# Branch B of a hybrid attention block: four heads of a key-value group in one value product, one transpose for their meta weights, one order of the keys

## The chip, the cores and the metric

The kernel runs on one core of one Trainium2 chip. The time is the device time of one execution in microseconds (us); the median of three runs before the change is 1888.18 us (1886.59 to 1889.76). A profile is one execution of the program taken by the hardware profiler. In it PE is TensorE (matmuls), PEld its weight loads, DVE is VectorE, ACT is ScalarE, POOL is GpSimd, and SP is SyncE, which issues the DMAs. L1261 is line 1261 of the kernel before.

## The reference

One encoder layer is applied to a prompt of 2048 tokens and a sample of 512, each with 16 learned meta tokens ahead of it. A projection gives queries, keys, values and gates for two attention branches. Branch A attends over a grid. Branch B is what changes here: windowed attention with eight query heads and two key-value heads, so that four query heads share one head's keys and values (a key-value group).

```python
s_band = einsum('bnqkgd,bnckd->bnkgqc', qr, k_band) * scale + band_bias    # 3 blocks of 128 keys
s_meta = einsum('bnqkgd,bmkd->bnkgqm', qr, km) * scale + meta_bias         # 16 meta keys
p = softmax(concatenate([s_band, s_meta, sink_col], axis=-1), axis=-1)     # a sink logit per head
o_real = (einsum('bnkgqc,bnckd->bnqkgd', p[..., :C], v_band)
        + einsum('bnkgqm,bmkd->bnqkgd', p[..., C:C + N_META], vm))
```

The output of each branch is multiplied by a gate, projected, gated again, added, and projected once more; a final norm follows.

## The kernel before

All numbers are float32. A matmul at this precision is made from a high and a low part of each operand (type fp32r, one pass of TensorE each): w = wh + wl, u = uh + ul, and wh·uh + wh·ul + wl·uh is summed in PSUM (mm3, lines L146 to L148). Splitting an operand is a cast on ScalarE (the high part) and a subtraction on VectorE or GpSimd (the low part).

Up to 985 us of the profile the kernel projects the input (line L848 above all). Then the attention stretch begins. It goes through five windows of 512 tokens (window 0 is the sample). In each window come 32 units of branch A, then 16 units of branch B. Units of B are the function unit_b(w, gh, n, i): window w, key-value group gh, query block n of 128 tokens, and i, which picks two of the group's four heads. Between the units' own instructions dense projections are put in to keep TensorE at work (the generators dense_pa, dense_pb, dense_out, last_gates; function fill), six matmuls of 512 columns at a time.

A unit is a generator of stages, and the loop at L1557 calls the stages of several units in turn. In a step of unit i it calls: the loads of unit i + 4; the scores of unit i + 2; the normalising of unit i + 1; some dense work; the transposes of unit i; some dense work; the value products of unit i - 1. TensorE's instructions stay in this order. The order on VectorE, ScalarE, GpSimd and SyncE is chosen by the framework's scheduler.

The stages of a B unit, for its two heads:

- Loads. The keys' tile kt has 18 columns ahead (16 meta keys, a column for the sink, a pad), then two or three blocks of 128, then the 16 meta keys once more. The bias tile has a copy of its first columns at its end too. The first query block of a sequence has a bias tile of its own (bb0).
- Scores. Two matmuls per head (L1217, L1218) into the PSUM tile s; VectorE adds the bias and takes the row maximum (L1042, two rows of the profile: the operation, and the read of its sum); ScalarE takes the exponential and its sum (L1049). Head 0 has its meta keys at the end, head 1 at the start, so that in the tile prs the two heads' meta columns lie side by side.
- Normalising. VectorE inverts the sums (L1053) and scales one head (L1060); ScalarE scales the other (L1058).
- Transposes. TensorE transposes each block of 128 keys of each head (L1237) and the 32 meta columns of the two heads together (L1240) into PSUM tiles tp. ScalarE casts them to the high part ph (L1244), VectorE subtracts for the low part pl (L1245). ph and pl have 14 places of 128 columns; alternate units use places 0 to 5 and 6 to 11. The meta weights go to a tile pms of 96 rows (high, low, high): two casts (L1254, L1256) and a subtraction (L1255).
- Value products. For each block of keys, a matmul of the high part (L1261; 256 columns, two heads of 128 queries; v holds 64 columns high and 64 low) and one of the low part (L1266). Ahead of the last low one stand the meta products (L1264), one per head, 128 columns each, with weights vms[:, gh, h, :] of 96 rows and 64 columns.
- The upper half of the sum is copied (L1268) and added to the lower (L1271) into y32. After block 3 GpSimd multiplies by the gate z (L1274), and y_split makes high and low parts.

Of the kernel before, what the change touches and what calls it, by code (L numbers as in the profile page):

```python
# [17 lines left out]
P = 128  # L18
# [77 lines left out]
def encoder_block(ctx: ExitStack, tc: tile.TileContext, xT, x_end, w_in, w_pa, w_pb, w_o, norm_g, final_g,  # L96
# [940 lines left out]
    HALF = 416  # L1037
# [31 lines left out]
    def unit_a(w, p, h, g, sh):  # L1069
# [49 lines left out]
        pr = at.tile([P, 2 * HALF], F32, tag="pr", name="pr", bufs=3)[:, :WTOK]  # L1119
# [45 lines left out]
    def unit_b(w, gh, n, i, sh):  # L1165
# [12 lines left out]
        if n == 0 and i == 0:  # L1178
            q = sh["q"] = ld.tile([P, 2, 2, WTOK], F32R, tag="q", name="q")
            for j in range(2):  # L1180
                move(q[:, j], qb_d[w, p + j].rearrange("(h d) i t -> (d i) h t", h=2))
            bt = sh["b"] = ld.tile([P, 2, 2, EXTRA + 3 * P + N_META], F32, tag="ba", name="bb")
            for j in range(2):
                move(bt[:, j, :, : EXTRA + 3 * P], bias_b[p + j])
                move(bt[:, j, 0, EXTRA + 3 * P :], bias_b[p + j][:, 0, :N_META])
        if n == 0 and first:
            bt0 = sh["b0", i] = ld.tile([P, 2, EXTRA + 2 * P + N_META], F32, tag="b0", name="bb0")
            move(bt0[:, :, : EXTRA + 2 * P], bias_b0[p])
            move(bt0[:, 0, EXTRA + 2 * P :], bias_b0[p][:, 0, :N_META])
# [3 lines left out]
        if i == 0:  # L1193
            kt = sh["k"] = ld.tile([P, 2, EXTRA + 3 * P + N_META], F32R, tag="kd", name="kbt")
            move(kt[:, :, EXTRA : EXTRA + nbk * P],
                 kb_d[gs].rearrange("d j i t -> (d j) i t")[:, :, b0 : b0 + nbk * P])
            move(kt[:, :, :EXTRA], kbm_d[gs].rearrange("d j i t -> (d j) i t"))
            move(kt[:, :, ncol : ncol + N_META], kbm_d[gs].rearrange("d j i t -> (d j) i t")[:, :, :N_META])
        kt, q, z = sh["k"], sh["q"][:, i], sh.get(("z", i))
# [3 lines left out]
        y32 = sh["y", i]  # L1203
        bt = sh["b0", i] if first else sh["b"][:, i]
        prs = at.tile([P, 2 * HALF], F32, tag="pr", name="prs", bufs=3)
        cols = slice(HALF - ncol, HALF), slice(HALF, HALF + ncol)
        k0 = HALF - ncol + EXTRA - N_META, HALF + EXTRA
        if nbk == 2 and not first:
            nc.vector.tensor_copy(bt[:, 0, ncol : ncol + N_META], bt[:, 0, :N_META])
        sm = sums_of()  # L1210
        for h in range(2):
            if h and (gh, n, i) == (0, 0, 0):
                yield
            s = ps_s.tile([P, WTOK], F32, tag="s", name="s")

            ks = slice(N_META * (1 - h), N_META * (1 - h) + ncol)
            nc.tensor.matmul(s[:, :ncol], q[:, h, qs], kt[:, 0, ks], start=True, stop=False)  # L1217
            nc.tensor.matmul(s[:, :ncol], q[:, h, qs], kt[:, 1, ks], start=False, stop=True)  # L1218
            nm = scores_max(s, ncol, bt[:, h, ks])
            exps(prs[:, cols[h]], s[:, :ncol], nm, sm[:, h : h + 1])  # L1220
        yield
        rd = inverse(sm)
        for h in range(2):
            normalise(prs[:, cols[h]], prs[:, cols[h]], rd[:, h : h + 1], on_act=h == 1)
        yield
        slots = [("k", j) for j in range(nbk)] + [("m", 0)]
        parts = []
        c0 = 6 * ((2 * n + i) % 2)
        for half in range(0, len(slots), 2):
            tp = ps_p.tile([P, WTOK], F32, tag="tp", name="tp")  # L1230
            part = slots[half : half + 2]
            nk = sum(1 for t, _ in part if t == "k")
            for m, (t, j) in enumerate(part):
                c = 2 * m * P
                if t == "k":
                    for h in range(2):
                        nc.tensor.transpose(tp[:, c + h * P : c + (h + 1) * P],  # L1237
                                            prs[:, k0[h] + j * P : k0[h] + (j + 1) * P], ident)
                else:
                    nc.tensor.transpose(tp[: 2 * N_META, c : c + P], prs[:, HALF - N_META : HALF + N_META], ident)  # L1240
            if nk:
                x = slice(c0 + 2 * half, c0 + 2 * half + 2 * nk)
                tb = tp[:, : nk * 2 * P].rearrange("p (b t) -> p b t", t=P)
                nc.scalar.copy(ph_[:, x], tb)  # L1244
                nc.vector.tensor_sub(pl_[:, x], tb, f32(ph_[:, x]))  # L1245
            for m, (t, j) in enumerate(part):
                c = slice(2 * m * P, 2 * (m + 1) * P)
                if t == "k":
                    x = slice(c0 + 2 * (half + m), c0 + 2 * (half + m) + 2)
                    parts.append((j, *(t[:, x].rearrange("p b t -> p (b t)") for t in (ph_, pl_))))  # L1250
                else:
                    pm = pms[(2 * n + i) % 2]
                    tm = tp[:32, c.start : c.start + P]
                    nc.scalar.copy(pm[0:32], tm)  # L1254
                    nc.vector.tensor_sub(pm[32:64], tm, f32(pm[0:32]))  # L1255
                    nc.scalar.copy(pm[64:96], f32(pm[0:32]))  # L1256
        yield
        o = ps_o.tile([P, WTOK], F32, tag="o", name="ob")
        for m, (j, hi, lo) in enumerate(parts):
            vb = sh["v"][:, (b0 - tlo) // P + j, :]  # L1260
            nc.tensor.matmul(o[:, : 2 * P], vb, hi, start=(m == 0), stop=False, skip_group_check=True)  # L1261
            if m == nbk - 1:
                for h in range(2):
                    nc.tensor.matmul(o[:64, h * P : (h + 1) * P], vms[:, gh, h, :], pms[(2 * n + i) % 2], start=False,  # L1264
                                     stop=False, skip_group_check=True)
            nc.tensor.matmul(o[:64, : 2 * P], vb[:, :64], lo, start=False, stop=m == nbk - 1, skip_group_check=True)  # L1266
        ol = at.tile([64, WTOK], F32, tag="ol", name="ol", bufs=1)[:, : 2 * P]
        nc.scalar.copy(ol, o[64:128, : 2 * P])  # L1268
        for h in range(2):
            hs = slice(64 * h, 64 * h + 64)  # L1270
            nc.vector.tensor_add(y32[hs, qs], o[:64, h * P : (h + 1) * P], ol[:, h * P : (h + 1) * P])  # L1271
        if n == 3:
            eng = nc.vector if w == NWIN - 1 and gh else nc.gpsimd
            eng.tensor_mul(y32, y32, z)  # L1274
            y_split("b", w, p, y32, eng)
# [253 lines left out]
    pms = [yp.tile([96, P], F32R, tag=f"pms{i}", name=f"pms{i}") for i in range(2)]  # L1529
    vms = yp.tile([96, 2, 2, 64], F32R, tag="vms", name="vms")  # L1530
# [3 lines left out]
    with tc.manual_schedule(engines={E.PE}):  # L1534
# [17 lines left out]
        vbm = vbm_d.rearrange("m g (h f) -> m g h f", h=2)  # L1552
        for h in range(2):
            for r, part in ((0, 0), (32, 0), (64, 1)):
                move(vms[r + 16 * h : r + 16 * h + 16, :, h], vbm[:, :, part, :])
        next(units[0][2])
        for i in range(N):  # L1557
# [12 lines left out]
            fill(share)  # L1570
            next(units[i][2])
# [3 lines left out]
            if i:  # L1575
# [111 lines left out]
```

## Time and profile before

| what | value |
|---|---|
| median of three runs | 1888.18 us |
| span of the profiled execution (first to last instruction) | 1881.7 us |
| what lies between the two | 6.5 us |
| TensorE busy | 1855.9 us, 99% |
| weight loads busy (beside the matmuls) | 1583.0 us, 84% |
| VectorE, ScalarE, GpSimd busy | 70%, 61%, 39% |
| granted TensorE clock | 0.999 of full |

The page has no time of its own for the profiled execution; its span stands 6.5 us under the median of the runs, and what lies around the span is the start and the end of the execution.

In a group's row stand: line, engine, operation, output tile <- input tiles, partitions x columns, the count; then busy us, mean ns of one; then the idle time of the engine just before them and what ended it. In a timeline row stand start, length, engine, line, operation, tiles, shape, and the count of like rows that were merged. In a row of waits stand the total in us, the times and the longest. TensorE pipelines its instructions and their ends are modelled, so that rows overlap one another and the mean of a group is longer than the distance between two starts.

### The profile page before, as it was taken

How to read it: one execution, taken by the hardware profiler on the slowest of the kernel's cores; microseconds unless marked ns; L12 is line 12 of the kernel's file. 1: busy time of each engine (PE TensorE's matmuls, PEld its weight loads, DVE VectorE, ACT ScalarE, POOL GpSimd, SP SyncE). 2: the span in 40 equal slices, each digit the busy share in tenths (PEclk: the TensorE clock that was granted, in tenths of full speed). 3: DMA queues.
4: the chain of work that ended last, by engine and by line, in shares of the span. 5: the costliest groups of instructions: out<-in, count | busy, mean ns of one | idle time of the engine just before them, and what ended most of it. 6: DMA issues, size and time to landing. Idle time of an engine off the chain costs nothing. (4 is left out here: it accounts for less than half of the span.)

```text
span 1881.7 us, 29782 instructions
## 1 busy us (share of the span) xinstructions
PE 1855.9 (99%) x9797; PEld 1583.0 (84%) x9797; DVE 1320.6 (70%) x2961; ACT 1145.5 (61%) x2528; POOL 730.0 (39%) x558
## 2 busy tenths in 40 slices
PE   8999999999999999999999999999999999999998
PEld 6898888888888888888888888888888888888887
DVE  8886657556477565444457888878787887888874
ACT  6454444444365443444456797797789788878932
POOL 2005443323202233322324435656744763685420
PEclk9999999999999999999999999999999999999999
DMA  7667756544296777744258878977985996798383
GB/s 268 234 175 295 207 171 193 211 175 179 84 348 219 235 216 200 209 138 161 104 197 310 273 217 266 304 213 249 316 280 179 320 315 225 222 311 260 119 299 135
DMA packets 290385, 424.83 MB, mean 226 GB/s; under 512 B 117416, under 2 KB 162040, under 8 KB 288696
## 3 DMA queue, kind: packets, MB, share of 16 engines
q1 hardware_dynamic: 289944, 422.93, 69.5%
q8 instruction: 78, 1.28, 0.3%
q14 instruction: 75, 0.61, 0.1%
q10 hardware_dynamic: 288, 0.01, 0.0%
HBM read 303.46 MB, written 119.39 MB: 225 GB/s over the span
## 5 line engine op out<-in xcount | busy, mean ns | idle before, releaser
L208 POOL TENSOR_TENSOR wt<-wraw,wt 128x512 fp32r<-128x512 f32 x164 | 213.1, 1318 | 265.9 <-ACT wt L207 265.8
L848 PE MATMUL pa<-u,wt 128*128 128x512 f32 x1008 | 242.5, 389 | 0.0
L848 PE MATMUL pa<-u,x 128*128 128x512 f32 x984 | 236.9, 390 | 1.2 <-ACT u L859 1.1
L207 ACT CAST wt<-wraw 128x512 fp32r<-128x512 f32 x312 | 177.9, 619 | 74.8 <-PE mm L148 35.3
L848 PEld LDWEIGHTS pa<-u,wt 128*128 128x128 f32 x1008 | 189.0, 188 | 39.2
L848 PEld LDWEIGHTS pa<-u,x 128*128 128x128 f32 x984 | 184.3, 188 | 40.6 <-ACT u L859 2.2
L819 POOL TENSOR_TENSOR s<-wraw,raw 128x512 f32<-128x512 f32 x40 | 58.3, 1458 | 265.5 <-DVE x L208 265.5
L146 PE MATMUL mm<-u,wt 128*128 128x512 f32 (+2 forms) x416 | 150.4, 362 | 7.8 <-ACT u L334 7.2
L814 POOL TENSOR_TENSOR s<-raw 128x512 f32<-128x512 f32 x40 | 58.3, 1456 | 250.0 <-DMA raw<-in_w_in_dram 245.0
L148 PE MATMUL mm<-u,wt 128*128 128x512 f32 (+2 forms) x416 | 146.6, 352 | 2.4 <-DVE wt L208 2.4
L147 PE MATMUL mm<-u,wt 128*128 128x512 f32 (+2 forms) x416 | 146.6, 352 | 1.3 <-DVE u L335 1.3
L208 DVE TENSOR_TENSOR wt<-wraw,wt 128x512 fp32r<-128x512 f32 x148 | 107.2, 762 | 47.2 <-ACT wt L207 47.0
L848 PE MATMUL pe<-u,wt 128*128 128x512 f32 x504 | 121.3, 390 | 0.0
L848 PE MATMUL pc<-u,wt 128*128 128x512 f32 x504 | 121.1, 389 | 0.0
L848 PE MATMUL pe<-u,x 128*128 128x512 f32 x480 | 115.3, 389 | 0.0
L848 PEld LDWEIGHTS pc<-u,wt 128*128 128x128 f32 x504 | 94.6, 188 | 19.6
L848 PEld LDWEIGHTS pe<-u,wt 128*128 128x128 f32 x504 | 94.4, 188 | 19.6
L1139 DVE TENSOR_TENSOR pl<-tp,ph 128x384 fp32r<-128x384 f32 (+6 forms) x160 | 94.8, 593 | 20.2 <-ACT ph L1138 17.7
L1138 ACT CAST ph<-tp 128x384 fp32r<-128x384 f32 (+6 forms) x160 | 81.7, 510 | 43.4 <-PE tp L1135 41.9
L146 PE MATMUL pso<-mh,wt 128*128 128x512 f32 x256 | 107.1, 418 | 0.0
L827 POOL TENSOR_TENSOR s<-wraw,s 128x512 f32<-128x512 f32 x40 | 55.4, 1384 | 131.6 <-DVE wt L208 126.3
L848 PEld LDWEIGHTS pe<-u,x 128*128 128x128 f32 x480 | 90.1, 188 | 18.7
(258 smaller groups left out, 5017.0 us busy)
## 6 DMA issues: line engine op xcount, KB each, us to landing
wraw<-in_w_in_dram SPq DMA_DIRECT2D x86, 512.0 KB
qa<-evq SPq DMA_DIRECT2D x20, 1024.0 KB
raw<-in_w_in_dram SPq DMA_DIRECT2D x40, 512.0 KB
q<-qa SPq DMA_DIRECT2D x20, 1024.0 KB
wraw<-in_w_o_dram SPq DMA_DIRECT2D x32, 512.0 KB
kbt<-kb SPq DMA_DIRECT2D x32, 384.0 KB
qb<-evq SPq DMA_DIRECT2D x20, 512.0 KB
ka<-evk SPq DMA_DIRECT2D x20, 512.0 KB
```

The lines of the kernel that those rows point to most:

```text
L146: nc.tensor.matmul(ps, wh, uh, start=first, stop=False)
L147: nc.tensor.matmul(ps, wh, ul, start=False, stop=False)
L148: nc.tensor.matmul(ps, wl, uh, start=False, stop=last)
L207: nc.scalar.copy(h, r)
L208: low[0] = (eng or lo_eng[0]).tensor_sub(l, r, f32(h)).ins
L814: eng.tensor_add(s1, a21, a22)
L819: eng.tensor_sub(s3, a11, a21)
L827: eng.tensor_sub(s4, a12, s2)
L848: nc.tensor.matmul(ps, wt[:, a, s], u[:, b, kk, :], start=first and kk == 0 and i == 0, stop=kk == 3 and i == 2, skip_group_check=True)
L1138: nc.scalar.copy(ph_[:kb, a], tb)
L1139: nc.vector.tensor_sub(pl_[:kb, a], tb, f32(ph_[:kb, a]))
```

## The change

- One order of keys for all heads. kt and the bias tile hold the 18 columns once, ahead of the blocks, or behind them in the first query block of a sequence, where the bias comes from the same tile's columns. The tile bb0 and the copies of meta columns go.
- Normalising scales the band columns only. A new GpSimd multiplication writes the two heads' normalised meta columns into the tile mt, which both units of a pair (i = 0 and 1) fill: four heads by 16 columns.
- Transposes. The band's stay. The meta weights of the four heads are transposed once, in the unit i = 1 (L1234 of the changed kernel). ph and pl are laid out by block, unit and head (four places per block, 12 in all for three blocks), with no second set. The meta weights go to a tile pms of 128 rows (64 high, 64 low) with one cast and one subtraction (L1242, L1243).
- Value products are made for four heads at once, in the unit i = 1 alone: 512 columns each (L1252, L1257). There are four meta products (L1255), one per head, each with weights vms[:, gh, m, :] of 128 rows and 128 columns, zero outside the head's rows.
- The loop takes the value products of unit i - 1 ahead of the transposes of unit i, wherever one of the two is a B unit.
- pms and vms move from one pool of SBUF to another; vms is cleared whole on GpSimd, and loaded by eight DMAs where there were six.

```diff
-            bt = sh["b"] = ld.tile([P, 2, 2, EXTRA + 3 * P + N_META], F32, tag="ba", name="bb")
+            bt = sh["b"] = ld.tile([P, 2, 2, HALF + EXTRA], F32, tag="ba", name="bb")
...
+            x = nbk * P + EXTRA if first else 0
+            move(kt[:, :, x : x + EXTRA], kbm_d[gs].rearrange("d j i t -> (d j) i t"))
...
+        ks, cols = (slice(x, x + ncol) for x in ((EXTRA, EXTRA + P) if first else (0, 0)))
+        band, meta = (slice(0, nbk * P), nbk * P) if first else (slice(EXTRA, ncol), 0)
...
         for h in range(2):
-            normalise(prs[:, cols[h]], prs[:, cols[h]], rd[:, h : h + 1], on_act=h == 1)
+            normalise(prs[:, h, band], prs[:, h, band], rd[:, h : h + 1], on_act=h == 1)
+        nc.gpsimd.tensor_mul(mt[:, 2 * i : 2 * i + 2, :], prs[:, :, meta : meta + N_META],
+                             rd[:, :, None].broadcast_to([P, 2, N_META]))
...
+            end = i == 1 and j0 + 2 > nbk
+            if end:
+                tm = tp[: 4 * N_META, 2 * nk * P : (2 * nk + 1) * P]
+                nc.tensor.transpose(tm, mt.rearrange("p n m -> p (n m)"), ident)
...
+            if end:
+                nc.scalar.copy(pms[:64], tm)
+                nc.vector.tensor_sub(pms[64:], tm, f32(pms[:64]))
         yield
+        if i == 0:
+            yield
+            return
...
+            nc.tensor.matmul(o, vb, hi, start=j == 0, stop=False, skip_group_check=True)
+            if j == nbk - 1:
+                for m in range(4):
+                    nc.tensor.matmul(o[:, m * P : (m + 1) * P], vms[:, gh, m, :], pms, start=False,
                                      stop=False, skip_group_check=True)
+            nc.tensor.matmul(o[:64], vb[:, :64], lo, start=False, stop=j == nbk - 1, skip_group_check=True)
...
-    pms = [yp.tile([96, P], F32R, tag=f"pms{i}", name=f"pms{i}") for i in range(2)]
-    vms = yp.tile([96, 2, 2, 64], F32R, tag="vms", name="vms")
+    pms = at.tile([P, P], F32R, tag="pms", name="pms", bufs=1)
+    vms = at.tile([P, 2, 4, P], F32R, tag="vms", name="vms", bufs=1)
...
+            early = i and "b" in (br, units[i - 1][0])
+            if early:
+                next(units[i - 1][2])
             next(units[i][2])
...
-            if i:
+            if i and not early:
                 next(units[i - 1][2])
```

Three places show how the order moves. The first is TensorE in window 2, group 0, from the transposes of the third block's unit i = 1 on. Before (pso is the dense work, ob the value products, s the scores):

```order
L1237 MATMUL tp<-ident,prs 128x128 x6
L1240 MATMUL tp<-ident,prs 32x128
...
L148 MATMUL pso<-mh,wt 128x512
L1261 MATMUL ob<-ph,vb 128x256
L1266 MATMUL ob<-pl,vb 64x256
L1261 MATMUL ob<-ph,vb 128x256
L1266 MATMUL ob<-pl,vb 64x256
L1261 MATMUL ob<-ph,vb 128x256
L1264 MATMUL ob<-pms_8528,vms 64x128 x2
L1266 MATMUL ob<-pl,vb 64x256
L1217 MATMUL s<-kbt,q 128x402
```

In the changed kernel:

```order
L1229 MATMUL tp<-ident,prs 128x128 x6
L1234 MATMUL tp<-ident,mt 64x128
...
L148 MATMUL pso<-mh,wt 128x512
L1209 MATMUL s<-kbt,q 128x402
...
L148 MATMUL pso<-mh,wt 128x512
L1252 MATMUL ob<-ph,vb 128x512
L1257 MATMUL ob<-pl,vb 64x512
L1252 MATMUL ob<-ph,vb 128x512
L1257 MATMUL ob<-pl,vb 64x512
L1252 MATMUL ob<-ph,vb 128x512
L1255 MATMUL ob<-pms,vms 128x128 x4
L1257 MATMUL ob<-pl,vb 64x512
L1229 MATMUL tp<-ident,prs 128x128 x6
```

The products that stood behind the transposes were those of the unit before; now the products that follow are those of the transposes' own pair, and they stand ahead of the next transposes.

The second place is VectorE after the same transposes. Before (s is the scores' tile of a later unit, y the head's output):

```order
L1245 TENSOR_TENSOR pl<-tp,ph 128x512
L1245 TENSOR_TENSOR pl<-tp,ph 128x256
L1255 TENSOR_TENSOR pms_8529<-tp,pms_8529 32x128
L1042 ISA s,nm<-s,bb 128x402
L1042 ISA nm 128x1
L1271 TENSOR_TENSOR y_14321<-ob,ol 64x128 x2
```

In the changed kernel:

```order
L1240 TENSOR_TENSOR pl<-tp,ph 128x2x256
L1240 TENSOR_TENSOR pl<-tp,ph 128x256
L1042 ISA s,nm<-s,bb 128x402
L1042 ISA nm 128x1
L1042 ISA s,nm<-s,bb 128x402
L1042 ISA nm 128x1
L1243 TENSOR_TENSOR pms<-tp,pms 64x128
L1340 TENSOR_TENSOR hT<-pso,xres 128x512
```

The subtraction for the meta weights stood right behind the pl of its unit; now two row maxima stand between.

The third place is GpSimd around the second multiplication of the same pair (wt is a dense weight, ssq a sum of squares). Before:

```order
L208 TENSOR_TENSOR wt<-wraw,wt 128x512 x2
L1353 TENSOR_TENSOR ssq<-ssq,xres 128x512
L208 TENSOR_TENSOR wt<-wraw,wt 128x512 x2
L1353 TENSOR_TENSOR ssq<-ssq,xres 128x512
L208 TENSOR_TENSOR wt<-wraw,wt 128x512 x2
```

In the changed kernel:

```order
L208 TENSOR_TENSOR wt<-wraw,wt 128x512
L1220 TENSOR_TENSOR mt<-prs,rd 128x32
L208 TENSOR_TENSOR wt<-wraw,wt 128x512
L1346 TENSOR_TENSOR ssq<-ssq,xres 128x512
L1220 TENSOR_TENSOR mt<-prs,rd 128x32 x2
L208 TENSOR_TENSOR wt<-wraw,wt 128x512 x2
L1346 TENSOR_TENSOR ssq<-ssq,xres 128x512
```

The new multiplications stand between the weights' subtractions, with others of them ahead in the queue.

More of the change, by code (lines that the diff above doesn't have):

```diff
@@ L1035, in encoder_block @@
     ys = {}
-    HALF = 416
+    HALF = EXTRA + 3 * P
     def scores_max(s, n, bias):
@@ L1225, in unit_b @@
         yield
[L1226 to L1229, printed above, removed]
+        for j0 in range(0, nbk + i, 2):
             tp = ps_p.tile([P, WTOK], F32, tag="tp", name="tp")
[L1231 to L1240, printed above, removed]
-            if nk:
[L1242 to L1256, printed above, removed]
@@ new lines, in unit_b @@
+            js = range(j0, min(j0 + 2, nbk))
+            nk = len(js)
+            for m, j in enumerate(js):
+                for h in range(2):
+                    nc.tensor.transpose(tp[:, (2 * m + h) * P : (2 * m + h + 1) * P],
+                                        prs[:, h, band.start + j * P : band.start + (j + 1) * P], ident)
+            end = i == 1 and j0 + 2 > nbk
+            if end:
+                tm = tp[: 4 * N_META, 2 * nk * P : (2 * nk + 1) * P]
+                nc.tensor.transpose(tm, mt.rearrange("p n m -> p (n m)"), ident)
@@ L1257, in unit_b @@
+            if nk:
+                ph, pl = (t[:, 4 * j0 : 4 * (j0 + nk)].rearrange("p (j i h) t -> p j i h t", i=2, h=2)[:, :, i]
+                          for t in (ph_, pl_))
+                tb = tp[:, : nk * 2 * P].rearrange("p (j h t) -> p j h t", h=2, t=P)
+                nc.scalar.copy(ph, tb)
+                nc.vector.tensor_sub(pl, tb, f32(ph))
+            if end:
+                nc.scalar.copy(pms[:64], tm)
+                nc.vector.tensor_sub(pms[64:], tm, f32(pms[:64]))
         yield
+        if i == 0:
+            yield
+            return
@@ L1258, in unit_b @@
         o = ps_o.tile([P, WTOK], F32, tag="o", name="ob")
-        for m, (j, hi, lo) in enumerate(parts):
+        for j in range(nbk):
             vb = sh["v"][:, (b0 - tlo) // P + j, :]
[L1261 to L1264, printed above, removed]
-                                     stop=False, skip_group_check=True)
-            nc.tensor.matmul(o[:64, : 2 * P], vb[:, :64], lo, start=False, stop=m == nbk - 1, skip_group_check=True)
@@ L1275, in unit_b @@
-            y_split("b", w, p, y32, eng)
+            for j in range(2):
+                y32 = sh["y", j]
+                eng.tensor_mul(y32, y32, sh["z", j])
+                y_split("b", w, p - 1 + j, y32, eng)
         yield
@@ L1551, in encoder_block @@
             pass
[L1552 to L1555, printed above, removed]
+        for m in range(4):
+            move(vms[N_META * m : N_META * (m + 1), :, m, :], vbm_d)
+            move(vms[64 + N_META * m : 64 + N_META * (m + 1), :, m, :64], vbm_d[:, :, :64])
         next(units[0][2])
```

44 lines of the change are left out of this document (17 added, 27 removed).

## The prediction

> **What bounds the kernel now.** I read the head of the page first, then who waits for whom in the attention stretch, then the groups by shape, and last the order of time around one block.
>
> ```profile
> span 1881.7 us, 29782 instructions
> PE 1855.9 (99%) x9797; PEld 1583.0 (84%) x9797; DVE 1320.6 (70%) x2961; ACT 1145.5 (61%) x2528; POOL 730.0 (39%) x558
> ```
>
> TensorE is busy for 99% of the span, so that only instructions taken from its stream, or waits put into it, can move the time. The waits of TensorE from 985 us (the first unit of attention) to the end:
>
> ```profile
> PE tp L1135 <- DVE pr L1060: 2.4, 3, 1.0
> PE s L1111 <- DMA kd<-kam: 0.9, 1, 0.9
> PE s L1217 <- ACT prs L1049: 0.6, 1, 0.6
> PE fin_v L170 <- DVE pms L1255: 0.6, 2, 0.3
> PE ob L1261 <- DVE y L1271: 0.5, 1, 0.5
> ```
>
> That is about 5 us in nearly 900, and of branch B's own instructions (L1217, L1261) only 1.1 us. So the answer must come from what one matrix instruction occupies. The means of a group (a transpose 272 ns, say) overlap one another; what counts is the distance between starts. Here are the groups for their counts, then a B unit of window 2 in order of time (start, length):
>
> ```profile
> L1237 PE MATMUL tp<-ident,prs 128*128 128x128 f32 x448 | 61.9, 272 | 0.0
> L1266 PE MATMUL ob<-pl,vb 128*64 128x256 f32 x224 | 60.0, 281 | 0.0
> L1264 PE MATMUL ob<-pms,vms 96*64 96x128 f32 x160 | 22.7, 223 | 0.0
> L1240 PE MATMUL tp<-ident,prs 128*32 128x128 f32 x80 | 21.8, 272 | 0.0
> ```
>
> ```profile
> 1415.81 0.82 PE L1237 MATMUL tp<-ident,prs 128*128 128x128 f32 x6
> 1416.47 0.27 PE L1240 MATMUL tp<-ident,prs 128*32 128x128 f32 x1
> 1416.49 0.49 PE L146 MATMUL pso<-mh,wt 128*128 128x512 f32 x1
> 1416.82 0.40 PE L147 MATMUL pso<-ml,wt 128*128 128x512 f32 x1
> ...
> 1417.75 0.39 PE L148 MATMUL pso<-mh,wt 128*128 128x512 f32 x1
> 1417.98 0.28 PE L1261 MATMUL ob<-ph,vb 128*128 128x256 f32 x1
> ...
> 1418.56 0.28 PE L1264 MATMUL ob<-pms,vms 96*64 96x128 f32 x2
> 1418.68 0.28 PE L1266 MATMUL ob<-pl,vb 128*64 128x256 f32 x1
> 1418.80 0.35 PE L1217 MATMUL s<-kbt,q 128*128 128x402 f32 x1
> ...
> 1419.54 0.39 PE L146 MATMUL pso<-mh,wt 128*128 128x512 f32 x1
> ...
> 1420.90 0.82 PE L1237 MATMUL tp<-ident,prs 128*128 128x128 f32 x6
> ```
>
> Distances read from it: 512 columns, 0.23 us (1417.75 to 1417.98, and 1.16 us for the five from 1416.82). 256 columns, 0.116 (five from 1417.98 to 1418.56 make 0.58). An L1264 of 128 columns, 0.06 (two from 1418.56 to 1418.68). A transpose: from 1415.81 to 1416.82 lie seven transposes and one matmul of 512 columns; 1.01 less 0.23 leaves 0.78, or 0.11 each, the narrow L1240 included.
>
> **The change on TensorE's stream.** There are 80 units in 40 pairs and 448 hi or lo products.
>
> 1. Transposes of meta weights: 80 become 40. 40 x 0.11 = 4.4 us less.
> 2. Value products: 448 of 256 columns become 224 of 512. A couple takes 2 x 0.116 = 0.232 now, and one of 512 takes 1.16 / 5 = 0.232. Wide and narrow matmuls cost the same per column here, so that merging them buys nothing. The rows are read to 0.01 in five, 0.002 each: 224 x 0.004 = 0.9 us either way.
> 3. Meta products: 160 before and 160 after, but the weights of each go from 64 columns to 128, and four with different weights stand one behind the other. No row shows a matmul of 128 columns that has to load 128 columns of weights under its predecessor of 128. The nearest rows are branch A's narrowest scores, whose weight loads (PEld) and matmuls start thus:
>
> ```profile
> 1012.97 0.19 PEld L1112 LDWEIGHTS s<-kd,q 128*128 128x128 f32 x1
> 1013.08 0.19 PEld L146 LDWEIGHTS mm<-u,wt 128*128 128x128 f32 x1
> 1013.19 0.19 PEld L147 LDWEIGHTS mm<-u,wt 128*128 128x128 f32 x1
> ```
>
> ```profile
> 1012.97 0.26 PE L1111 MATMUL s<-kd,q 128*128 128x216 f32 x1
> 1013.18 0.40 PE L146 MATMUL mm<-u,wt 128*128 128x512 f32 x1
> ```
>
> Two matmuls of 216 columns take 0.21 us; by columns (0.23 x 216/512 = 0.097 each) they would take 0.19. The loads stand 0.11 apart: the full load sets the pace. For the loads of 64 columns the pace is 0.06 or less. So four meta products cost 4 x 0.06 = 0.24 per pair now, and then 3 x 0.11 + 0.06 = 0.39 (the last hides the load for a lo product, which stays at 64 columns): 0.15 x 40 = 6.0 us more. Bounds: nothing more, if such loads hide (a gain of the step itself is excluded, as the count and columns stay), and 4 x 0.05 x 40 = 8 us, if the fourth pays too. I take 6.0, as the row of the full load is nearest.
>
> The Trainium skill, page "TensorE: Matmul & The Clock Gate", section "Weight-path perf modes — Fast Weight Load (FWL) and DoubleRow", says that a load of a full 128 columns is sped up by itself where the type isn't FP32. By that rule the sum of the three steps would be -4.4 us. The loads above, a full 128 columns and still 0.11 apart, speak against it.
>
> Sum of the stream: -4.4 + 0 + 6.0 = +1.6 us. The price of one step is a little over the gain of another.
>
> **What leaves the other engines.** 120 instructions around the meta weights go from ScalarE and some 40 from VectorE:
>
> ```profile
> L1256 ACT CAST pms<-pms 32x128 fp32r<-32x128 f32 x80 | 23.7, 297 | 2.2
> L1254 ACT CAST pms<-tp 32x128 fp32r<-32x128 f32 x80 | 20.3, 254 | 12.1 <-DVE pl L1245 11.3
> L1255 DVE TENSOR_TENSOR pms<-tp,pms 32x128 fp32r<-32x128 f32 x80 | 22.4, 280 | 9.2 <-ACT pms L1254 7.0
> ```
>
> Some 34 us of ScalarE and 11 of VectorE; neither bounds, so this buys only earlier evictions. The fewer small loads are worth nothing: the one wait for a DMA above is branch A's. SyncE's queue loses rows and gains only the two more loads of vms, issued once. The larger clear of vms stands on GpSimd here:
>
> ```profile
> 976.77 0.31 POOL L1531 MEMSET vms<- 96x256 f32 x1
> 982.10 2.74 POOL L208 TENSOR_TENSOR wt<-wraw,wt 128x512 fp32r<-128x512 f32 x2 [5.02 <-ACT wt L207]
> ```
>
> Four times its columns would be some 1.3 us, in 5 us of idle time.
>
> **Waits that it may add.** The order has two sides. Products of a pair now stand ahead of the next transposes, and there is one set of ph and pl. The copy into them waits for products that stand ahead of its own transposes on TensorE anyway, so that the reuse costs nothing. But the distance from a pair's last transpose to its products shrinks. By the rows above it was: transposes at 1416.47, the next transposes at 1420.90, and the unit's products behind them and six more matmuls, 1420.90 + 0.78 + 6 x 0.23 = 1423.1, 6.6 us. It becomes 1.49 (1416.49 to 1417.98) + 0.74 (scores, 1418.80 to 1419.54) + 1.36 (1419.54 to 1420.90) = 3.6 us; the meta products come five matmuls later, at 4.75. Behind a late product wait all later dense work and transposes. VectorE's rows for the same unit:
>
> ```profile
> 1418.27 1.02 DVE L1245 TENSOR_TENSOR pl<-tp,ph 128x512 fp32r<-128x512 f32 x2 [0.30 <-ACT ph L1244]
> 1419.61 0.28 DVE L1255 TENSOR_TENSOR pms<-tp,pms 32x128 fp32r<-32x128 f32 x1 [0.32 <-ACT pms L1254]
> ...
> 1420.90 0.57 DVE L1042 CUSTOM_DVE_ANT_0 s<-s,bb 128x402 f32<-128x402 f32 x1
> 1421.49 0.08 DVE L1042 DVE_READ_ACCUMULATOR2_ANT nm<- 128x1 f32 x1
> ```
>
> pl is done 2.82 us after the transpose. In the new order two row maxima (0.67 each, 1420.90 to 1421.57) stand ahead of the meta weights' subtraction: 2.82 + 1.34 + 0.28 = 4.44, against a need at 4.75: hidden, with 0.3 us to spare. In the last window VectorE runs later:
>
> ```profile
> 1726.85 0.27 PE L1240 MATMUL tp<-ident,prs 128*32 128x128 f32 x1
> 1730.83 0.41 DVE L1245 TENSOR_TENSOR pl<-tp,ph 128x256 fp32r<-128x256 f32 x1
> 1732.65 0.28 DVE L1255 TENSOR_TENSOR pms<-tp,pms 32x128 fp32r<-32x128 f32 x1
> ```
>
> There pl ends at 4.39; with one maximum behind it the meta weights are there at 5.34, 0.6 late. Eight pairs of that window would make 4.8 us; none would be 0. I take 1.0, as both engines lose work. The wait of 0.5 us of L1261 goes, since the final products come later.
>
> The new multiplication for mt stands in GpSimd's queue behind weight subtractions. At the place shown in the order it stands behind this one:
>
> ```profile
> 1403.96 1.43 POOL L1353 TENSOR_TENSOR ssq<-ssq,xres 128x512 f32<-128x512 f32 x1
> ```
>
> That ends at 1405.39, and the transpose that would wait comes at 1416.47: 11 us of cover. If the cover were gone, a pair would lose about one such subtraction, 1.3 us. Its own time lies between 0 and 1.43 us, off the path.
>
> At the end of attention two heads' y finish together, one more multiplication and split on VectorE, while TensorE has dense work queued; I put it at 0 to 1 us, and take 0.
>
> **Sum.** +1.6 + 1.0 - 0.5 = +2.1 us. The page has the span of 1881.7 and no time of its own execution; the median of the runs, 1888.2, lies 6.5 us above it, work outside the span that the change doesn't touch. 1888.2 + 2.1 = 1890.3. A measurement of this kernel can tell about 0.2%, 3.8 us, from no change.
>
> **The rivals.**
>
> A, slower: the meta weights come late. The place is the subtraction behind two maxima on VectorE, and it decides from 0.3 us of delay. For it: the row of the last window, where the old subtraction ended 1732.93 - 1726.85 = 6.1 after the transpose, 1.3 beyond the new need. Against: the steady rows, and the instructions that go. If the eight pairs of that window lose 1.3 each, and the other 32 no more than 0: +1.6 + 10.4 - 0.5 = +11.5, 1899.7; with half of those waits 1894.5.
>
> B, faster: the meta products' loads hide. Then step 3 is 0, the stream is -4.4, and with 0.5 us of waits added and 0.5 gone the time is 1883.8. The skill's rule above is this case. For it: nothing shows four such loads in this type. Against: the 0.11 between full loads.
>
> C: mt is late on GpSimd, as a queue held up by a weight that waits for its DMA would make it. Every pair losing 1.3 us makes 52 us, 1940. Against: 11 us of cover.
>
> That the change doesn't do what it says is excluded for the counts: the order shows one meta transpose and four products in a pair.
>
> **How the numbers follow.** Forecast 0.54, A 0.27, B 0.15, C 0.04. The range takes in B (1883.8, and the 0.9 of step 2) and the milder half of A: 1883 to 1897. Faster by over 0.2% (below 1884.4) is B, and a little of the forecast, if part of the loads hides: 0.16. Slower (above 1892.0) is A and C, less A's mildest part: 0.29. Within: 0.55.
>
> **What would show it.** Right: one meta transpose less per pair; four meta products in 0.35 to 0.45 us, their loads 0.11 apart; products of 512 columns 0.23 apart; waits of the new products on VectorE of 0 to 5 us in all. Wrong: meta products 0.06 apart (B); waits of the products for pms or pl over 5 us, in the last window above all (A); transposes of mt that wait for GpSimd (C).

## The result and the profile after

| | us | ratio to the kernel before, on record |
|---|---|---|
| before | 1889.25 median (1886.59 to 1890.27, 5 runs) | |
| after | 1893.84 median (1892.58 to 1897.01, 5 runs) | ratio 1.0034, 95% interval 1.0021 to 1.0047 |
| after, timed once more (e5) | 1893.70 median (1893.18 to 1896.98, 5 runs) | ratio 1.0034, 1.0022 to 1.0047 |

The change makes the kernel slower: by the ratio, 0.0034 x 1888 = 6.4 us. The ratios on record aren't the quotients of two medians: the medians of the first two rows stand 4.6 us apart, and e5's stands 6.0 us above that of the nine runs of the kernel before that were timed beside it. The forecast was 1890.3, in a range of 1883 to 1897. The head of the page after:

```profile
span 1890.7 us, 29050 instructions
PE 1862.2 (98%) x9533; PEld 1572.7 (83%) x9533; DVE 1318.3 (70%) x2913; ACT 1108.5 (59%) x2368; POOL 747.8 (40%) x638
```

ScalarE loses 37 us of busy time, which is no gain by itself, as TensorE still bounds. TensorE's waits from 985 us to the end, in the columns of before (total, times, longest):

```profile
PE ob L1255 <- DVE pms L1243: 2.8, 4, 1.8
PE s L1209 <- ACT prs L1049: 1.9, 3, 0.8
PE tp L1229 <- DVE pl L1240: 1.5, 1, 1.5
...
PE ob L1257 <- DVE pl L1240: 0.6, 2, 0.3
```

The meta products wait for pms four times, and there are waits for pl. Where? In the table by stretches stand the stretch, its length and TensorE's busy time in it; then the weight loads, VectorE, ScalarE and GpSimd, the granted clock, the DMA engines' share and GB/s. The rows are the B stretches of the first, third and last window before, and of all five windows after:

```profile
1064.00:1143.40 79.40, 78.73 (x484) 68.53 (x483) 66.11 (x206) 67.88 (x189) 27.98 (x22) 1.00 0.79 242
...
1382.40:1474.30 91.90, 91.61 (x563) 81.20 (x562) 73.56 (x216) 79.89 (x207) 46.67 (x37) 1.00 0.71 226
...
1714.40:1801.10 86.70, 86.19 (x531) 75.83 (x531) 72.99 (x210) 73.32 (x194) 39.80 (x31) 1.00 0.51 154
```

```profile
1065.30:1147.20 81.90, 78.72 (x428) 65.03 (x427) 62.75 (x189) 59.19 (x154) 31.24 (x37) 1.00 0.69 219
1221.30:1309.30 88.00, 87.83 (x485) 74.78 (x484) 69.10 (x201) 68.19 (x169) 48.26 (x52) 1.00 0.67 223
1386.30:1476.70 90.40, 90.39 (x498) 77.23 (x497) 72.18 (x205) 70.79 (x173) 48.41 (x52) 1.00 0.66 220
1553.70:1643.60 89.90, 89.90 (x497) 77.08 (x496) 71.72 (x205) 70.49 (x173) 48.11 (x51) 1.00 0.65 213
1718.50:1810.10 91.60, 87.75 (x479) 73.07 (x478) 68.34 (x195) 65.92 (x162) 43.40 (x47) 1.00 0.47 145
```

Length less busy time is TensorE's idle time: after, 3.2 us in the first window, 0.2, 0 and 0 in the three between, 3.9 in the last. Before it was 0.7, 0.3 and 0.5 in the rows shown. So the three middle windows bear the change all but without a wait, and the first and the last together idle 5.9 us more (2.5 + 3.4).

The price of the meta products stands in the timeline of one pair in the third window:

```profile
1420.42 0.27 PE L1234 MATMUL tp<-ident,mt 128*64 128x128 f32 x1
...
1424.05 0.40 PE L1252 MATMUL ob<-ph,vb 128*128 128x512 f32 x1
1424.29 0.40 PE L1257 MATMUL ob<-pl,vb 128*64 128x512 f32 x1
...
1425.22 0.56 PE L1255 MATMUL ob<-pms,vms 128*128 128x128 f32 x4
1425.62 0.39 PE L1257 MATMUL ob<-pl,vb 128*64 128x512 f32 x1
```

Four meta products take 0.40 us from the first start to the next instruction (1425.22 to 1425.62), where two pairs of the old ones took 2 x 0.12 = 0.24. The products of 512 columns stand 0.23 to 0.24 apart. The first product comes 3.63 us after the last transpose, and the meta products at 4.80. On VectorE, in the same pair:

```profile
1421.42 1.01 DVE L1240 TENSOR_TENSOR pl<-tp,ph 128x512 fp32r<-128x512 f32 x2
...
1423.71 0.28 DVE L1243 TENSOR_TENSOR pms<-tp,pms 64x128 fp32r<-64x128 f32 x1
```

The meta weights are there at 1423.99, 3.6 us after their transpose and 1.2 ahead of their use.

In the pair of the longest wait, in the last window, the lateness begins on ScalarE. The transpose of the meta weights starts at 1771.52 there. Their cast ends 5.75 us later, at 1777.27, behind two exponentials (the second is shown). VectorE is idle for 1.55 us until that exponential's sum is there, and subtracts behind an inverse and a scaling:

```profile
1776.44 0.60 ACT L1049 ACTIVATE prs<-s,nm 128x402 f32<-128x402 f32 x1
...
1777.01 0.26 ACT L1242 CAST pms<-tp 64x128 fp32r<-64x128 f32 x1
...
1777.17 0.17 DVE L1053 RECIPROCAL rd<-sm 128x2 f32<-128x2 f32 x1 [1.55 <-ACT prs L1049]
...
1777.95 0.28 DVE L1243 TENSOR_TENSOR pms<-tp,pms 64x128 fp32r<-64x128 f32 x1
...
1778.29 0.66 PE L1255 MATMUL ob<-pms,vms 128*128 128x128 f32 x4 [1.82 <-DVE pms L1243]
```

### The profile page after: what moved, and what is told of

Read it like the earlier page. It is cut to its first block, busy times and chain, and to the rows that moved or that the text cites. A ratio compares the mean times of both kernels' runs of the same rounds, so it can differ in the third digit from the quotient of the medians.

```text
span 1890.7 us, 29050 instructions
## 1 busy us (share of the span) xinstructions
PE 1862.2 (98%) x9533; PEld 1572.7 (83%) x9533; DVE 1318.3 (70%) x2913; ACT 1108.5 (59%) x2368; POOL 747.8 (40%) x638
## 5 line engine op out<-in xcount | busy, mean ns | idle before, releaser
L1049 ACT ACTIVATE prs<-s,nm 128x402 f32<-128x402 f32 (+1 forms) x160 | 91.2, 575 | 55.0 <-DVE nm L1042 45.8
L1042 DVE CUSTOM_DVE_ANT_0 s<-s,ba 128x384 f32<-128x384 f32 (+5 forms) x160 | 86.9, 543 | 31.9 <-PE s L1112 29.0
```

Source lines behind the costliest of these rows:

```text
L1042: nc.vector.tensor_tensor_reduce(s[:, :n], s[:, :n], bias, -1.0, 3.0e38, ALU.add, ALU.min, nm)
L1049: nc.scalar.activation(out, s, AF.Exp, bias=nm, scale=-1.0, accum_out=sm)
```

## The experiments

The theory after the result had two parts: the stream is some 2 us dearer, as forecast, and the rest is waiting in the first and the last window. The rivals were that the loads alone, or late meta weights alone, are the loss.

**e1, the kernel before again.** No edit.

> The kernel before, unchanged, against itself. It tells how far a second profile of it lies from the first (span 1881.7 us, five waits of about 5 us in attention) and what lies between span and time. Both theories: ratio 1.000, within 0.15%. If the first profile was a fast execution, this span is 1883 to 1888 us and the difference of the spans of after and before (9.0 us) shrinks towards the difference of the medians (4.6 us).

Measured: ratio 1.000 (0.999 to 1.0011, 12 runs against 17). The profiled execution took 1894.24 us with a span of 1892.2, so that 2.0 us lie around the span. The first profile's span of 1881.7 therefore belonged to an execution of about 1884 us, under all the runs shown with it. The expected 1883 to 1888 for this span was a miss: this execution has long waits in branch A that the first lacks (its waits; the longest of the first profile was 1.0):

```profile
PE tp L1135 <- DVE pr L1060: 7.2, 4, 2.1
```

A single profile is thus good to about 5 us either way, and totals of two profiles can't be set against one another. But the stretch from the last score matmul of branch A to the end of the program, worked out from the starts in the trace, is 169.2 us in one and 169.3 in the other. Such stretches are compared below.

**e2, meta products of 64 columns.**

```diff
-nc.tensor.matmul(o[:, m * P : (m + 1) * P], vms[:, gh, m, :], pms, start=False,
+nc.tensor.matmul(o[:64, m * P : (m + 1) * P], vms[:, gh, m, :64], pms, start=False,
```

> The changed kernel with the meta products cut to 64 columns of weights; it leaves out the product of the high part of the meta weights with the low part of the meta values. Theory 1 (the loads of 128 columns set the pace of the meta products, 0.11 us each in the trace after): the four products take 4 x 0.06 = 0.24 us in place of 0.06 + 3 x 0.11 = 0.39, 0.15 x 40 = 6 us less than the changed kernel, 1888 us, a ratio to the kernel before of 0.999. Rival (the loss is all wait for late weights, and the loads would hide): no more than 1 us less, 1893 us, ratio 1.002 to 1.0035, products still 0.11 apart.

Measured: 1895.40 us, ratio 1.0037 (1.0024 to 1.0049). The sum of the distances from a meta product to what follows it fell from 16.7 to 10.0 us over the 160, as theory 1 said, and the time did not. About half of what it brought was given back in the first window of this kernel's profile: the wait for pl grew from 1.5 to 2.2 us, some 3 us at a lower clock followed it (last section), and two new waits came behind it.

```profile
PE tp L1229 <- DVE pl L1240: 3.5, 3, 2.2
PE ob L1255 <- DVE pms L1243: 2.8, 5, 1.6
```

By the starts in the trace, the stretch from branch A's last score matmul in a window to its next one takes 75.4 us in the first window, where the changed kernel takes 73.2. In the third it is 78.9 in place of 79.6, and from the last score matmul of branch A to the end 173.4 in place of 174.2, so that the gain does show there. Where the rest of it went isn't shown. Neither theory had this; the likely reason is that a faster TensorE only arrives earlier at a wait on VectorE.

**e3, the meta transpose first.** The unit i = 1 fills the tile of the third block first, the meta transpose ahead of the block's two, with pms evicted ahead of ph and pl; the products take the blocks in the order third, first, second.

```diff
-        for j0 in range(0, nbk + i, 2):
+        for j0 in (range(0, nbk, 2) if i == 0 else (2, 0)):
...
+            if end:
+                tm = tp[: 4 * N_META, 2 * nk * P : (2 * nk + 1) * P]
+                nc.tensor.transpose(tm, mt.rearrange("p n m -> p (n m)"), ident)
+                nc.scalar.copy(pms[:64], tm)
+                nc.vector.tensor_sub(pms[64:], tm, f32(pms[:64]))
```

> The changed kernel with the meta transpose as the first of the unit's transposes, its cast and subtraction written ahead of the band's, the tile with the third block next, and the value products in the order third, first, second block, meta ahead of the last low part. The same work. Theory 1: the waits of the meta products for pms (2.8 us in the waits of the trace after, 4.0 us in the distances) go, the loads stay at 0.11: 3 to 4 us less, 1890 us, ratio 1.0005 to 1.002. Rival (late weights are all of the loss): 4.6 us less, ratio 1.000. Third view (the low part pl comes late in place of pms, being behind pms now): waits for pl of 2 us or more take their place and the ratio stays at 1.003.

Measured: 1944.07 us, ratio 1.0304 (1.0277 to 1.0331). No view had this, and it tells nothing on the change. The edit added a wait of its own: the block's transposes go to the tile from which VectorE still has to read the meta weights (the waits, and the place in one pair).

```profile
PE tp L1235 <- DVE pms L1232: 44.3, 32, 3.0
```

```profile
1419.36 0.87 PE L1235 MATMUL tp<-ident,prs 128*128 128x128 f32 x6 [1.94 <-DVE pms L1232]
```

**e4, meta products spread.**

```diff
+        for j in order_:
+            nc.tensor.matmul(o, vbs[j], hi[j], start=j == order_[0], stop=False, skip_group_check=True)
+        seq = [x for m in range(4) for x in (("m", m), ("l", m))]
+        for kind, m in seq:
...
```

> The changed kernel with the same value products in another order: the high parts of all blocks, then by turns a meta product and a low part, so that the load of 128 columns for a meta product runs under a product of 512 columns and only one or two of the loads have a matmul of 128 columns ahead. Theory 1: meta products cost 4 x 0.06 and 0.05 to 0.1 for the one that another load follows at once, 0.30 to 0.34 us in place of 0.39; 0.05 to 0.09 x 40 = 2 to 4 us less on the stream; but pms is needed 0.47 us earlier (two low parts of 0.23 us come later), which in the last window and where a sequence starts gives back up to 8 x 0.47 x 2 = 4 us. Ratio 1.001 to 1.0035. Rival (loads cost nothing): no gain, and the earlier need costs 1 to 4 us: ratio 1.004 to 1.0055.

Measured: 1898.90 us, ratio 1.0052 (1.0039 to 1.0065). The number is the rival's. Its waits are the cause: the meta products (L1257 here), which are needed earlier, wait 7.0 us in all, nine times, where the changed kernel's waited 2.8. That the loads still gain shows in the third window, whose stretch is 79.0 us in place of 79.6.

```profile
PE ob L1257 <- DVE pms L1243: 7.0, 9, 2.1
```

**e5, the changed kernel again.**

> The changed kernel, unchanged, beside the other three. Both theories: ratio 1.0034 as in its first timing, within 0.13%, and in the trace the waits in the same two stretches, the first and the last window of branch B, 3 to 5 us in each by the distances of starts, and the three windows between them within 1 us of the kernel before.

Measured: the ratio of the table above, and the same waits, 2.9 us of the meta products for pms and 1.5 us of the transposes for pl. From the last score matmul of branch A to the end it takes 174.2 us in both profiles of it, against 169.2 and 169.3 of before. So 5.0 us of the loss lie in the last window and what follows it, and they repeat.

**e6, the kernel before with the new order of stages alone.**

```diff
+            early = i and "b" in (br, units[i - 1][0])
+            if early:
+                next(units[i - 1][2])
             next(units[i][2])
...
-            if i:
+            if i and not early:
```

> The kernel before with one part of the change alone: the value products of unit i - 1 stand ahead of the transposes of unit i wherever one of the two is a unit of branch B. Two-head units, two sets of ph and pl, and two-head meta transposes stay; so TensorE's stream has the same instructions, and only the distance from the transposes to their own products shrinks, from 6.6 to 3.6 us. Theory 1 (after the second set of runs: the loss is waiting in the first and the last window, because of this distance): 3 to 8 us of new waits, ratio 1.002 to 1.004. Rival (the loss is in the stream of the four-head form): ratio 1.000, waits as before.

Measured: 1937.96 us, ratio 1.0266 (1.0252 to 1.0280), 50 us slower, with the same instructions on TensorE. The cause is theory 1's, the size is six times the upper end: every window waits, not the first and the last.

```profile
PE ob L1264 <- ACT pms L1256: 22.7, 18, 2.4
PE ob L1264 <- DVE pms L1255: 12.0, 14, 1.1
```

In one unit of the fourth window, ScalarE has the meta weights' second cast behind two exponentials and a scaling, and TensorE waits 1.48 us for it:

```profile
1606.14 0.60 ACT L1049 ACTIVATE prs<-s,nm 128x402 f32<-128x402 f32 x1
...
1606.94 0.60 ACT L1049 ACTIVATE prs<-s,nm 128x402 f32<-128x402 f32 x1
...
1607.53 0.24 ACT L1254 CAST pms<-tp 32x128 fp32r<-32x128 f32 x1
1607.86 0.63 ACT L1058 ACTIVATE prs<-prs,rd 128x402 f32<-128x402 f32 x1
1608.52 0.29 ACT L1256 CAST pms<-pms 32x128 fp32r<-32x128 f32 x1
```

```profile
1608.87 0.34 PE L1264 MATMUL ob<-pms,vms 96*64 96x128 f32 x2 [1.48 <-ACT pms L1256]
```

So the order that the change brings costs 50 us by itself, in the form with two heads. Most of that is absent in the changed kernel, which has one cast and one subtraction per pair in place of six instructions, and products after every second unit only. Which of the two takes it away isn't shown, as no run has one without the other.

**e7, the tile with the meta weights first, without e3's wait.** As e3, but with the meta transpose behind the third block's two.

```diff
+            if i == 1 and j0 == 2:
+                tm = tp[: 4 * N_META, 2 * nk * P : (2 * nk + 1) * P]
+                nc.tensor.transpose(tm, mt.rearrange("p n m -> p (n m)"), ident)
+                nc.scalar.copy(pms[:64], tm)
+                nc.vector.tensor_sub(pms[64:], tm, f32(pms[:64]))
```

> The changed kernel with the tile that holds the third block and the meta weights filled and evicted first (the meta weights' eviction first of all), then the tile with the first two blocks; the value products go third, first, second block with the meta products in the last. The same work, and no transpose into a tile that is being read. Theory 1: the waits of the meta products for pms go (2.8 us in the trace after), those for pl may grow by up to that much, since pl of the last tile ends 0.3 us later than now: ratio 1.001 to 1.0035. Rival (late meta weights are all of the loss): ratio 1.000.

Measured: 1898.46 us, ratio 1.0051 (1.0037 to 1.0065), slower than either view. No wait for pms is left, but pl is late instead (L1256 is a low product here):

```profile
PE ob L1256 <- DVE pl L1241: 4.2, 9, 1.3
```

Late meta weights are thus not the whole: in this order pl is evicted last, and pl is late.

**e8, more dense work behind the second transposes.**

```diff
-            fill(share)
+            first = br == "b" and i % 2 == 0
+            fill(share * (1 if br == "a" else 1.5 if first else 0.5))
...
-            fill(share)
+            fill(share * (1 if br == "a" else 0.5 if first else 1.5))
```

> The changed kernel with the dense work of branch B shared out differently, the same in all: half a share between a pair's two sets of transposes on either side, one and a half on the other two sides. So the value products stand six matmuls of 512 columns (1.4 us) further behind their own pair's last transposes, and the two sets of transposes 1.4 us nearer to one another. Theory 1 (distance): the waits for pms and pl, 2.8 + 0.6 + 1.5 us in the trace after, fall under 1.5 us, ratio 1.000 to 1.002. Rival (distance plays no part): ratio 1.003 to 1.004. Third view (the second transposes of a pair then come too early for their tiles and normalised weights): waits of the transposes on VectorE and ScalarE, ratio over 1.004.

Measured: 1907.55 us, ratio 1.0105 (1.0091 to 1.0119), the third view. The waits for pms fall to 0.2 us, as the theory of distance says. But the transposes of the unit i = 1 now come too early for their tiles:

```profile
PE tp L1229 <- DVE pl L1240: 15.9, 21, 1.4
...
PE ob L1255 <- DVE pms L1243: 0.2, 1, 0.2
```

TensorE's waits at these transposes also give VectorE time, so that the fall to 0.2 us over the whole attention isn't the distance's alone. The last window is the cleaner case: its transposes wait 1.1 us in all, no meta product waits, and the last stretch falls from 174.2 to 172.3 us.

**e9 to e12, the dense shares levelled.** What the first and the last window have in common stands in the plan: branch B gets 27 and 30 portions of six dense matmuls there, and 32 in the other windows (COUNT, line 1494 of the changed kernel). Counted in the order, two pairs of the first and one of the last window have 6 dense matmuls between their last transposes and their products where the others have 12 (the last pair of a window apart). A portion is missing at the first window's longest wait too: there the transposes of a pair's second unit, which wait 1.5 us for pl, stand 6 dense matmuls behind those of the first unit, where the third window has 12. The short pair of the last window, as the changed kernel has it:

```profile
1762.09 0.27 PE L1234 MATMUL tp<-ident,mt 128*64 128x128 f32 x1
...
1764.35 0.41 PE L1252 MATMUL ob<-ph,vb 128*128 128x512 f32 x1
1765.09 0.45 PE L1257 MATMUL ob<-pl,vb 128*64 128x512 f32 x1 [0.34 <-DVE pl L1240]
...
1765.96 0.66 PE L1255 MATMUL ob<-pms,vms 128*128 128x128 f32 x4 [0.18 <-DVE pms L1243]
```

Its products come 2.26 us behind the transposes, not 3.63. The edit of e9, and of e10 on the kernel before:

```diff
-    GATES_0, GATES_A, HELD = 8, 40, 5
+    GATES_0, GATES_A, HELD = 8, 35, 5
...
-    COUNT = {("a", 0): GATES_A, ("b", 0): 80 - GATES_0 - GATES_A - HELD, ("b", NWIN - 1): 30}
+    COUNT = {("a", 0): GATES_A, ("b", 0): 80 - GATES_0 - GATES_A - HELD, ("b", NWIN - 1): 32}
```

> The changed kernel with the dense shares of branch B levelled: 35 gate columns in branch A of the sample in place of 40 (which leaves 32 for its branch B in place of 27), and 32 in place of 30 for branch B of the last window. Every pair but the last of a window then has 12 dense matmuls between its last transposes and its products; in the changed kernel two pairs of the first window and one of the last have 6, and there the distance is 2.0 to 2.8 us in place of 3.6. Theory (the waits come where the distance is shortest): the waits of those three pairs go, about 1.2 us in the first window and 0.9 in the last by the distances of starts, and some of the others behind them: 2 to 4 us less, ratio 1.0012 to 1.0025. Rival (the waits come from VectorE's and ScalarE's load in these windows, whatever the distance): ratio 1.0034 as it stands.

> The kernel before with the same levelling. Theory: its products stand 6.6 us behind their transposes and do not wait, so nothing is gained: ratio 1.000, within 0.1%. If it gains as much as the changed kernel does, levelling is worth something by itself, and e9 says nothing on the distance.

Measured: e9 1888.20 us, ratio 1.0007 (0.9997 to 1.0016); e10 1888.34 us, ratio 1.000 (0.999 to 1.0009), 12 runs each. The same edit gives nothing to the kernel before, whose last stretch stays at 169.2 us, and takes 0.0027 x 1888 = 5.1 us from the changed one, more than the 2 to 4 expected. All of e9's waits on TensorE from 985 us on:

```profile
PE s L1209 <- ACT prs L1049: 2.0, 2, 1.5
PE s L1111 <- DMA kd<-kam: 1.3, 1, 1.3
PE fin_v L170 <- DVE pl L1240: 0.8, 1, 0.8
PE oa L1152 <- DVE pl L1139: 0.2, 1, 0.2
```

No product and no transpose of branch B waits any more. The last stretch takes 169.7 us, 4.5 less than 174.2. In the first window the waits for pl and pms go too, but a wait of 1.5 us for the scores' tile comes at the border to branch B (e10 has it there too), so that the gain is the last window's. The longest wait of the changed kernel, 1.82 us in the pair behind the short one, went as well, though that pair had 12 dense matmuls all along; that it was the short pair's consequence wasn't tried by itself, and the edit also shifts the dense work of the pairs behind it.

A short distance isn't enough for a wait, however. The last pair of each of the three middle windows has 6 dense matmuls as well, and its products come 1.9 to 2.0 us behind the last transposes, in the changed kernel and in e9. None of them waits. Branch A's units follow there; whether this is what spares them wasn't tried.

e11 is e9 with e2's edit, e12 is e9 with e4's.

> The levelled changed kernel with the meta products cut to 64 columns of weights; it leaves out the product of the high part of the meta weights with the low part of the meta values. In the second run this cut took 6.7 us from the distances of the meta products and nothing from the time. Theory (what it took was given back in the first window, as waits and, behind the longest of them, a lower granted clock): without those waits it is 4 to 6 us under the levelled kernel, ratio 0.998 to 1.000. Rival (VectorE and ScalarE set the pace of branch B whatever TensorE saves): within 1 us of the levelled kernel.

> The levelled changed kernel with the exact value products in the order of the fourth run: high parts, then meta products and low parts by turns, so that most loads of 128 columns run under 512 columns. Theory: 0.05 to 0.1 us per pair less on the stream, 2 to 4 us, and with 3.6 us of distance pms is there in the windows between (3.6 us after the transposes against a need at 4.3), while the last window still waits: 0 to 3 us under the levelled kernel, ratio 1.000 to 1.0025. Rival (the earlier need decides, as in the fourth run): 2 to 4 us over the levelled kernel.

Measured: e11 1885.73 us, ratio 0.9989 (0.9980 to 0.9998); e12 1886.01 us, ratio 0.9997 (0.9988 to 1.0007). With the waits gone the loads do show: e11 is 0.0018 x 1888 = 3.4 us under e9, short of the 4 to 6 expected. e12 is 0.0010 x 1888 = 1.9 under it, in the range, but each of the two ratios is known to about 0.001, so that the times alone don't show a gain. The stretches do: the third window's takes 79.6 us in e9, 78.9 in e11 and 79.0 in e12, and the last one 169.7, 168.1 and 168.3. Their pairs in the third window, e11 and then e12 (whose L1257 is the meta product and L1261 the low one):

```profile
1426.35 0.40 PE L1255 MATMUL ob<-pms,vms 128*64 128x128 f32 x4
1426.58 0.40 PE L1257 MATMUL ob<-pl,vb 128*64 128x512 f32 x1
```

```profile
1422.92 0.22 PE L1257 MATMUL ob<-pms,vms 128*128 128x128 f32 x1
1422.98 0.40 PE L1261 MATMUL ob<-pl,vb 128*64 128x512 f32 x1
```

With 64 columns of weights, four take 0.23 us in place of 0.40. With 128 columns whose load runs under 512 columns, one takes 0.06. From the first product to the next transposes a pair of e12 takes 1.64 us and one of the changed kernel 1.80, so that a pair gains 0.16, more than the 0.05 to 0.1 expected. e12 computes all and is, by its ratio, the best exact form of the change here; its interval holds no change, so that nothing here beats the kernel before but e11, which leaves work out.

## Why the prediction was right, and which of its steps was not

- **Direction and size.** A stream a little dearer, some waits in the last window, 1890.3 in a range to 1897: measured 1893.8. The range held it; the slower half of it was the true one. By the prediction's own division that time counts as slower (above 1892.0), which had a chance of 0.29, and not as the forecast. Of its signs of being right, the counts, the 0.40 us of the meta products and the new products' waits of 3.4 us in all (2.8 and 0.6) came.
- **Transposes, -4.4 us.** As forecast: 40 transposes go, and those left still stand 0.11 apart.
- **Merged products, 0.** As forecast: 0.23 us for 512 columns, where two of 256 took 0.232.
- **Meta products, +6.0 us.** The row gives 0.40 in place of 0.24 us, 0.16 x 40 = 6.4. The load of 128 columns sets the pace, as the row of branch A had said, and rival B is out. If the first of the four takes the 0.06 us of its columns, (0.40 - 0.06) / 3 = 0.11 is left for each that stands behind a load, as far apart as branch A's full loads. The Trainium skill's page "TensorE: Matmul & The Clock Gate" (section "Weight-path perf modes — Fast Weight Load (FWL) and DoubleRow") speeds up full loads of types other than FP32, and says that FP32 gains nothing. These fp32r weights, 0.11 us apart, show no such gain.
- **Waits, +1.0 us less 0.5.** This is the term that failed, in its size: TensorE idles 5.9 us more in the first and the last window. The step that failed was the distance. It was read from one pair of a middle window, 3.6 us, and taken for all pairs; the plan gives the first and the last window fewer portions of dense work, three pairs have 2.0 to 2.8 us, and e9 shows that with all portions in place the waits are gone (the last pairs of the middle windows are as short and don't wait, so that the distance isn't the whole condition). The lateness was also put on VectorE alone: the cast on ScalarE had no term, and in the longest wait it ended only 5.75 us after the transpose. The estimate for the middle windows was too cautious instead: 0.3 us to spare forecast, 1.2 measured.
- **Rival A**, with half of its waits 1894.5, came nearest in time. Its place, meta weights that come late in the last window, is right. Its path is not the whole: in the longest wait ScalarE is late ahead of VectorE. The first window wasn't in it, nor the missing portions, and pl waits beside pms.
- **Rival C**, mt late on GpSimd: no transpose of mt waits in the trace. Out.
- **The new order.** Its price of "3.6 us where it was 6.6" was taken as nearly free. e6 shows that with two-head units it costs 50 us alone, more than any other part. "Neither bounds, so this buys only earlier evictions" was too light a weight for what leaves ScalarE and VectorE: together with the rarer products, these fewer evictions are what the changed kernel has and e6 lacks, and most of the 50 us is absent there. How much of that is the evictions' doing isn't shown.
- **Around the span** lie 1.9 us (1892.58 less 1890.7), not 6.5, as the first profile was of an execution shorter than the runs shown. The forecast started from the median, so nothing hung on it.

Open is why e11 gains 3.4 us where its distances gain 6.7; in its profile 2.0 us of waits of the transposes for pl have come back, and for 3.4 us in the second window the granted clock was 0.50 (last section), which costs about half of that time. In this one execution the two would make up the rest; what the other runs of e11 have isn't shown.

## What to carry to other kernels

When a change shortens the distance between a producer and its consumer, read the distance where it is shortest, not in the steady state: count the filler between the two for every block, the first and the last stage above all, and level it there. An order of stages and the number of evictions are best priced together: here the order alone cost 50 us with two-head units, and the whole change, with fewer evictions, some 6. And weights that are widened cost by their load only where a narrow matmul runs ahead of them: put a wide one there.

## What the runs showed of the hardware

A wait of TensorE can cost more than its length. In e2 it stands empty from 1088 to 1090 us, and the granted clock (the first number behind the five engines' groups) is 0.50 from 1091 to 1094:

```profile
1088.00:1090.00 2.00, 0.01 (x1) 0.04 (x1) 1.98 (x7) 1.62 (x5) 0.00 (x0) 1.00 0.56 145
...
1091.00:1094.00 3.00, 3.00 (x10) 2.52 (x10) 1.78 (x6) 0.83 (x3) 0.16 (x1) 0.50 0.34 123
```

The matmuls of 512 columns there stand about 0.43 us apart in place of 0.23, and four score matmuls of 274 columns 0.23 in place of 0.13: some 1.5 us lost in all. In the changed kernel the wait of 1.82 us is followed by a clock of 1.00:

```profile
1776.00:1778.30 2.30, 0.48 (x4) 0.05 (x2) 0.93 (x3) 1.89 (x5) 2.02 (x3) 1.00 0.12 16
1778.30:1780.00 1.70, 1.70 (x13) 1.58 (x14) 0.09 (x1) 0.75 (x2) 0.00 (x0) 1.00 0.84 323
```

The length alone doesn't decide it: the 2.4 us of e6's longest wait weren't followed by a lower clock, the 2.2 us of e2 were. In e11 two waits of only 0.5 and 0.3 us, at 1282.5 and 1283.4, were followed by this:

```profile
1284.70:1288.10 3.40, 3.40 (x11) 2.90 (x10) 1.98 (x12) 0.59 (x2) 0.12 (x1) 0.50 0.45 164
```

The Trainium skill's page "TensorE: Matmul & The Clock Gate", section "Part 1: The HAM clock gate (the "warmup" mystery)", has a clock of half or full by the engine's activity in windows of about 3.4 us that run on freely. The 0.50 over some 3 us agrees with that. A wait that counts or not by where it falls would agree with it too, but no run here shows where such windows lie.
